# Twelve seven-product pairs instead of sixteen in a two-row-block encoder layer, with the norm's squares, the first loads and the last rows in another order

## The chip, the cores and the metric

The kernel runs on one core of a Trainium2 chip, as one program in one launch. The metric is the device time of that program in microseconds (us), and lower is better. A run of this kernel can be told from another when they differ by about 0.2%, some 2.7 us.

## The reference

The layer works on x, 256 positions of 2048 channels, in float32:

```python
def mixer_block(x, g_norm, w_in, ln_g, ln_b, w_s, b_s, rpb, w_branch, w_out):
    h = rms_norm(x, g_norm)
    proj = h @ w_in
    uv, qkv, gates = jnp.split(proj, [2 * GM_WIDTH, 2 * GM_WIDTH + 3 * NA_WIDTH], axis=-1)
    ...
    return x + merged @ w_out

def conv_ffn(x, g_norm, w_up, conv_k, conv_b, w_down):
    h = rms_norm(x, g_norm)
    up = h @ w_up
    ...
    gate, val = jnp.split(up, 2, axis=-1)
    return x + (jax.nn.silu(gate) * val) @ w_down

def reference(x, norm_mix, ...):
    ...
    return rms_norm(x, norm_final)
```

What matters here is that every matrix product is float32, that the mixer's norm scales its rows by a factor which is known only when the squares of x are summed, that the feed-forward part has 5504 inner channels (43 tiles of 128), and that a last norm over all 2048 channels of a row comes before the output.

## The kernel before, in words

**Products.** TensorE (PE) takes reduced-precision operands, so each float32 operand is split into a high and a low part: ScalarE (ACT) writes the high part (`high`, line 244) and VectorE (DVE) the rest (`low`, line 247). A product is then three matmuls, high by high, low by high and high by low (`three_products`, lines 381 to 383; `spread_products`, lines 366 and 372, is the same for weights that stand still). The weights come as one stream of packed pieces of 128 x 1024 from HBM, all on SyncE's (SP's) queue, through five raw buffers (`RAW`), and four, later six, buffers of split weights (`UNITS`). Piece i + 4 is prepared at the beginning of step i (`begin`, `prepare`) when a buffer is free. The first 16 pieces also carry a 128 x 256 part of x, turned, in four buffers of their own.

**Order of the work.** Each engine executes what the program emits, in that order. A step i of the loop emits the loads that have a free buffer, the splits of the pieces ahead, the tasks that were put down for step i with `at`, and then the matmuls of piece i. So a split that stands behind a task on ACT or DVE waits for that task.

**Start.** The group `vg` (16 pieces, `first_step`, lines 398 to 401) makes v of the gMLP branch in four PSUM banks; at its end four gelu activations (line 634) read these banks, with the rows' factor of the norm as their scale. That factor comes from `x_norm`, put down for step 15, after eight square sums (line 1163) in steps 11 to 14, of x rows that are loaded behind piece 15. Then follow the groups `u` (two of eight pieces).

**Feed-forward.** It is done in two blocks of 22 and 21 inner tiles. In a block, the `up` groups make pairs of inner tiles; a convolution, the gate and a split into high and low parts follow on DVE and ACT, as tasks of the next steps. Then two `down` groups (j = 0, 1), each of 22 or 21 pieces, multiply them by `w_down` into 1024 columns each.

**Seven products for eight.** Two neighbouring pieces of a `down` group are a 2 x 2 block product (two inner tiles by two column halves, for two halves of the positions): eight products. For some pairs (`FF_SEVEN`: 1, 3, 5 and 7, counted in pairs from the group's beginning, in both blocks) it is done with seven, by sums and differences of the operands. The sums of the weights are made by DVE: four additions of 128 x 512 (lines 293, 300, 303 and 304), between the splits. `sums` emits a pair's preparation in four parts, `one` to `four`, and `plan` puts the last two behind the first part of the next piece. The split operands are a half (128 x 512, `halves`), and three units: `b`, the second piece as it came, `t` and `s`, sums. The first step of a pair (9 matmuls) uses the half and `t`, the second (12 matmuls) uses `s` and `b`. After the last pair `combine` (line 475) folds four banks into x2, all at once.

**End.** The last three pieces of the last group are done block by block (`LAST`): for each of the four 128 x 512 blocks of the result all its remaining matmuls, so that blocks are complete one after the other. `finish` (line 1098) adds the last block of a row half to x2, sums its squares, makes the norm's factor, scales the 2048 columns in five parts and stores them; first for rows 0 to 127, then for rows 128 to 255.

Of the kernel before, what the change touches and what calls it, by code (L numbers as in the profile page):

```python
# [46 lines left out]
FF_SEVEN = (1, 3, 5, 7)  # L47
LAST = 3
# [101 lines left out]
def trunk_kernel(ctx, tc, x, weights, vectors, ln_g, ln_b, w_s_turned, b_s, rpb, norm_final, out):  # L150
# [62 lines left out]
    def load():  # L213
        while n_loaded[0] < len(pieces):
# [66 lines left out]
    def sums(i):  # L281
# [4 lines left out]
        def one():  # L286
# [3 lines left out]
            r0 = raw[i][0]  # L290
# [4 lines left out]
        def two():  # L295
            r0, r1 = raw[i][0], raw[i + 1][0]
            hb, lb = unit((i, "b"))
            ht, lt = unit((i, "t"))
            high(hb, r1)
            nc.vector.tensor_add(r0[:, c1], r0[:, c1], r1[:, c1])  # L300
            high(ht, r0)
            low(lb, r1, hb)
            nc.vector.tensor_add(r1[:, c1], r1[:, c1], r0[:, c0])
            nc.vector.tensor_add(r1[:, c0], r1[:, c0], r1[:, c1])
            low(lt, r0, ht)
            raw_done(i)

        def three():
            r1 = raw[i + 1][0]
            h, l = unit((i, "s"))  # L310
            high(h, r1)

        def four():
            r1 = raw[i + 1][0]
            h, l, _ = units[i, "s"]
# [3 lines left out]
        return one, two, three, four  # L319
# [4 lines left out]
    def plan():  # L324
        late = None
        i = 0
        while i < len(pieces):
            if i in seven:
                one, two, three, four = sums(i)
                if late:  # L330
                    queue.append((i, 1, 0, late[0]))
                queue.append((i, 0, 1, one))
                if late:
                    queue.append((i, 0, 0, late[1]))
                queue.append((i + 1, 2, 0, two))
                late = (three, four)
                i += 2
                continue
            if late:
                queue.append((i, 1, 0, late[0]))  # L340
            queue.append((i, 1, 0, split_piece(i)))
            if late:
                queue.append((i, 0, 0, late[1]))
            late = None
            i += 1
        if late:
            queue.extend([(i, 1, 0, late[0]), (i, 0, 0, late[1])])
# [37 lines left out]
    def first_step(key, acts, done):  # L385
# [3 lines left out]
        def step(i):  # L389
# [13 lines left out]
            if last:  # L403
                for b in range(NT):
                    for c in range(2):
                        done(box["ps"][2 * b + c], b, c, i + 1)
                        free(box["ps"][2 * b + c])
# [36 lines left out]
    def wide_step(key, acts, sevens, rest, done, by_block=0):  # L444
# [9 lines left out]
        while n < size:  # L454
            if n in firsts:
                uses += [1, 5, 7, 6, 2, 3, 4]
# [18 lines left out]
        def combine():  # L475

            nu, nv = (fx["p"].tile([128, 512], F32, name=f"comb{n}") for n in range(2))
            nc.scalar.activation(nu, p(1), AF.Copy)
            rest(0, 0, nu, OP.add)
            nc.vector.tensor_sub(nu, nu, p(6))  # L480
            nc.vector.tensor_sub(nv, nu, p(7))
            rest(0, 1, nu, OP.subtract)
            rest(0, 1, p(5), OP.add)
            rest(1, 0, nv, OP.add)
            rest(1, 1, nv, OP.subtract)
            rest(1, 1, p(5), OP.add)
            free(p(1), p(6), p(7), p(5))

        def step(i):
            n = i - n0  # L490
            c0, c1 = slice(0, 512), slice(512, 1024)
            if n in firsts:
                k = tiles[n]
                h, l, _ = halves[i]
                ht, lt, _ = units[i, "t"]
                S = sevens(k)
                product(1, acts(k, 0), (h, l))
                product(5, S[0], (ht[:, c0], lt[:, c0]))
                product(7, S[2], (ht[:, c1], lt[:, c1]))
                unit_done((i, "t"))  # L500
                half_free.append(halves.pop(i)[2])
            elif n - 1 in firsts:
                k = tiles[n - 1]
                hb, lb, _ = units[i - 1, "b"]
                hs, ls, _ = units[i - 1, "s"]
                S = sevens(k)
                product(6, S[1], (hs[:, c1], ls[:, c1]))
                product(2, acts(k + 1, 0), (hb[:, c0], lb[:, c0]))
                product(3, S[3], (hb[:, c1], lb[:, c1]))
                product(4, acts(k + 1, 1), (hs[:, c0], ls[:, c0]))  # L510
                unit_done((i - 1, "b"))
                unit_done((i - 1, "s"))
                if n - 1 == firsts[-1]:
                    combine()
# [6 lines left out]
            elif n == size - 1:  # L521
                for c in range(2):
                    for b in range(NT):
                        for m in range(size - by_block, size):
                            h, l, _ = units[n0 + m]
                            cs = slice(c * 512, (c + 1) * 512)
                            product(OUT[b, c], acts(tiles[m], b), (h[:, cs], l[:, cs]))
                        done(p(OUT[b, c]), b, c, i + 1)
                        free(p(OUT[b, c]))
# [27 lines left out]
    ck = vec[:, 2 * KD:].rearrange("p (j f) -> p j f", j=4)  # L557
    nc.scalar.dma_start(gmix, vectors[:, :KD])
# [68 lines left out]
    def ev_vg():  # L627
        def done(p, t, j, i):
            G = gm_pool["p"]
            if "v" not in gm_pool:  # L630
                gm_pool["v"] = [G.tile([128, GMW], F32, name=f"vg{b}") for b in range(NT)]
                gm_pool["sum"] = const.tile([128, NT, 2], F32, name="vsum")
                at(i + 1, ln_stats)
# [667 lines left out]
```

## Time and profile before

| | |
|---|---|
| three runs | 1343.62, 1345.53 and 1345.92 us; median 1345.53 us |
| the profiled execution's own time | 1345.03 us |
| its span in the trace | 1342.9 us |
| mean clock granted to TensorE | 0.993 |
| PE busy | 1312.0 us (98%) |
| DVE busy | 966.9 us (72%) |
| ACT busy | 736.0 us (55%) |
| the `down` groups | 854.06 to 972.99 us, and 1206.82 us to the last matmul |

The times of the trace count from the span's beginning, and 2.1 us of the profiled execution lie outside the span. A row of the timeline gives start, duration, engine, line and operation, output and inputs (buffer numbers left out) and, in brackets, how long the engine stood idle before it and what ended that. Rows of matmuls overlap: what a matmul costs in a stream is the distance of the starts, not the duration shown.

### The profile page before, as it was taken

How to read it: one execution, taken by the hardware profiler on the slowest of the kernel's cores; microseconds unless marked ns; L12 is line 12 of the kernel's file. 1: busy time of each engine (PE TensorE's matmuls, PEld its weight loads, DVE VectorE, ACT ScalarE, POOL GpSimd, SP SyncE). 2: the span in 40 equal slices, each digit the busy share in tenths (PEclk: the TensorE clock that was granted, in tenths of full speed). 3: DMA queues.
4: the chain of work that ended last, by engine and by line, in shares of the span. 5: the costliest groups of instructions: out<-in, count | busy, mean ns of one | idle time of the engine just before them, and what ended most of it. 6: DMA issues, size and time to landing. Idle time of an engine off the chain costs nothing.

```text
span 1342.9 us, 18498 instructions
## 1 busy us (share of the span) xinstructions
PE 1312.0 (98%) x6766; PEld 1117.6 (83%) x6766; DVE 966.9 (72%) x1397; ACT 736.0 (55%) x1082; POOL 96.5 (7%) x190
## 2 busy tenths in 40 slices
PE   9999999999999999999999999989999999998986
PEld 7788888888888888888888888878888888886865
DVE  6387667777564546555878787899867878779886
ACT  6655567576544444545655555554545555555453
POOL 0411065430000000000000000000000000000000
PEclk9999999999999999999999999999999999999988
DMA  8866776645666668565656565466756565655552
GB/s 301 315 188 195 212 221 188 198 155 184 188 187 190 193 193 265 193 197 167 191 189 189 192 191 189 145 204 190 248 177 199 180 199 183 187 167 172 202 172 95
DMA packets 74187, 261.41 MB, mean 195 GB/s; under 512 B 9584, under 2 KB 11248, under 8 KB 73584
## 3 DMA queue, kind: packets, MB, share of 16 engines
q1 hardware_dynamic: 69984, 252.40, 59.3%
q0 software_dynamic: 3680, 7.30, 2.1%
q8 instruction: 53, 0.87, 0.3%
q10 hardware_dynamic: 432, 0.53, 0.1%
q14 instruction: 38, 0.31, 0.1%
HBM read 256.00 MB, written 2.10 MB: 192 GB/s over the span
## 4 chain that ended last, share of the span: by engine, by line
PE 91%; DVE 4%; ACT 2%; issue 1%; DMA 1%; SPq 0%; DVEq 0%; ACTq 0%
PE bank L366 29%; PE bank L372 15%; PE bank L383 14%; PE bank L381 14%; PE bank L382 14%; DVE wlo L247 2%; PE bank L398 1%; PE bank L401 1%; PE bank L399 1%; ACT whi L244 1%; PE bank L835 1%; DMA start<-in_weights_dram 0%; DMA wraw<-in_weights_dram 0%; ACT junk L1074 0%; DVE x L969 0%
## 5 line engine op out<-in xcount | busy, mean ns | idle before, releaser
L247 DVE TENSOR_TENSOR wlo<-wraw,whi 128x1024 fp32r<-128x1024 f32 (+1 forms) x470 | 564.4, 1217 | 226.9 <-ACT whi L244 219.3
L244 ACT ACTIVATE whi<-wraw 128x1024 fp32r<-128x1024 f32 (+1 forms) x470 | 484.2, 1046 | 273.7 <-PE bank L382 151.6
L366 PE MATMUL bank<-h,whi 128*128 128x512 f32 x1760 | 424.8, 392 | 0.0
L366 PEld LDWEIGHTS bank<-h,whi 128*128 128x128 f32 x1760 | 323.9, 189 | 62.0
L372 PEld LDWEIGHTS bank<-h,wlo 128*128 128x128 f32 x1760 | 226.8, 191 | 11.5 <-DVE wlo L247 2.5
L372 PE MATMUL bank<-h,wlo 128*128 128x256 f32 x1760 | 231.4, 284 | 2.3 <-DVE wlo L247 2.3
L383 PE MATMUL bank<-wlo,a 128*128 128x512 f32 x312 | 123.4, 396 | 11.9 <-DVE wlo L247 11.9
L381 PE MATMUL bank<-whi,h 128*128 128x512 f32 x320 | 126.0, 394 | 0.0
L381 PE MATMUL bank<-whi,a 128*128 128x512 f32 x312 | 122.8, 393 | 3.1 <-ACT whi L244 2.9
L383 PE MATMUL bank<-wlo,h 128*128 128x512 f32 x320 | 124.8, 390 | 0.0
L382 PE MATMUL bank<-whi,h 128*128 128x512 f32 x320 | 124.7, 390 | 0.0
L382 PE MATMUL bank<-whi,a 128*128 128x512 f32 x312 | 122.2, 392 | 0.0
L1025 ACT ACTIVATE tc<-ta,vec 128x256 f32<-128x256 f32 x86 | 47.1, 594 | 88.0 <-DVE ta L1023 88.0
L701 DVE TENSOR_TENSOR ta<-bank,tb 128x256 f32<-128x256 f32 x110 | 39.0, 416 | 64.1 <-ACT tb L699 64.1
L699 ACT ACTIVATE tb<-bank 128x256 f32<-128x256 f32 x110 | 36.2, 384 | 89.1 <-PE bank L366 83.3
L383 PEld LDWEIGHTS bank<-wlo,a 128*128 128x128 f32 x312 | 59.1, 189 | 27.5 <-DVE wlo L247 15.4
L381 PEld LDWEIGHTS bank<-whi,a 128*128 128x128 f32 x312 | 59.2, 190 | 16.2 <-ACT whi L244 3.9
L383 PEld LDWEIGHTS bank<-wlo,h 128*128 128x128 f32 x320 | 60.1, 188 | 12.7
L381 PEld LDWEIGHTS bank<-whi,h 128*128 128x128 f32 x320 | 60.2, 188 | 12.2
L382 PEld LDWEIGHTS bank<-whi,h 128*128 128x128 f32 x320 | 60.2, 188 | 11.9
L382 PEld LDWEIGHTS bank<-whi,a 128*128 128x128 f32 x312 | 59.1, 189 | 12.3
L1028 DVE SCALAR_TENSOR_TENSOR tc<-ta,vec,tc 128x255 f32<-128x255 f32 x86 | 41.4, 481 | 14.4 <-ACT tc L1025 14.4
(169 smaller groups left out, 1321.5 us busy)
## 6 DMA issues: line engine op xcount, KB each, us to landing
wraw<-in_weights_dram SPq DMA_DIRECT2D x446, 512.0 KB, 4.4
start<-in_weights_dram SPq DMA_DIRECT2D x15, 640.0 KB, 6.0
xs<-in_x_dram SPq DMA_DIRECT2D x2, 1024.0 KB, 9.2
vw<-va POOLq DMA_DIRECT2D x32, 64.0 KB, 5.9
x<-in_x_dram POOLq DMA_DIRECT2D x2, 1024.0 KB, 9.7
wraw<-in_weights_dram SPq DMA_DIRECT2D x8, 256.0 KB, 2.7
run<-in_rpb_dram POOLq DMA_DIRECT2D x64, 31.2 KB, 3.9
h<-in_norm_final_dram POOLq DMA_DIRECT2D x4, 256.0 KB, 5.6
```

The lines of the kernel that those rows point to most:

```text
L244: nc.scalar.activation(h, w, AF.Copy)
L247: nc.vector.tensor_sub(l, w, h.bitcast(F32))
L366: nc.tensor.matmul(p, h[:, c:c + 128], acts(2 * n + k), start=n == 0 and k == 0, stop=last and k == tiles - 1)
L372: nc.tensor.matmul(p[:, :T], l[:, c:c + 128], acts(2 * n + k)[:, 0, :], start=False, stop=False)
L381: nc.tensor.matmul(p, xh, wh, start=start, stop=False)
L382: nc.tensor.matmul(p, xl, wh, start=False, stop=False)
L383: nc.tensor.matmul(p, xh, wl, start=False, stop=stop)
L398: nc.tensor.matmul(p, xh, h[:, cs], start=n == 0, stop=False)
L699: nc.scalar.activation(t, p[:, T:], AF.Copy)
L701: nc.vector.tensor_add(a, p[:, :T], t)
L1025: nc.scalar.activation(v, u, AF.Identity, scale=ck[:, 1, ch:ch + 1], bias=ck[:, 3, ch:ch + 1])
L1028: nc.vector.scalar_tensor_tensor(v[:, 1:], u[:, :T - 1], ck[:, 0, ch:ch + 1], v[:, 1:], op0=OP.mult, op1=OP.add)
```

## The change

Line numbers in the parts that follow the diff are those of each kernel; in the changed kernel `low` is line 248 and `high` line 245.

- `FF_SEVEN` gives each block its own three pairs: (3, 5, 7) in the first, (2, 4, 6) in the second. With two groups per block that is 12 pairs instead of 16; pairs 0 and 1 of a group are now never among them.
- A pair's preparation has three parts in plain order: `plain` (the half and `b`, as they came), `summed` (all four additions, then `t`) and `last` (`s`). The first step of a pair now uses the half and `b` (products 1, 2, 3), the second uses `t` and `s` (products 5, 7, 6, 4).
- `combine` is spread over the three steps behind the last pair. The tiles of split activations with and without sums have their own names.
- x's rows are loaded ahead of pieces 8 and 9 instead of behind piece 15. The squares are eight tasks of steps 6 to 13, one each, and `x_norm` is put down for step 14. The four gelu activations are put down for steps 16 and 17, two each.
- The loads of the first pieces are emitted ahead of the norm's weights; piece 0 comes in three parts, and its part of x is issued by ACT, ahead of the norm's weights on that queue.
- `LAST` is 4. `finish` is written anew: what is left of rows 0 to 127 is scaled among the steps of rows 128 to 255, two multiplications by the norm's weights go to GpSimd (POOL), and the output goes out in seven parts.

```diff
-FF_SEVEN = (1, 3, 5, 7)
-LAST = 3
+FF_SEVEN = ((3, 5, 7), (2, 4, 6))
+LAST = 4
...
-            for c0, c1 in ((0, 768), (768, 1280)) if i == 0 else ((0, size),):
-                nc.sync.dma_start(w[:, c0:c1], bass.AP(tensor=weights.tensor, offset=weights.offset + off + c0,
+            for c0, c1 in ((T, 768), (0, T), (768, 1280)) if i == 0 else ((0, size),):
+                queue = nc.scalar if (i, c0) == (0, 0) else nc.sync
+                queue.dma_start(w[:, c0:c1], bass.AP(tensor=weights.tensor, offset=weights.offset + off + c0,
...
+        def plain():
+            r0, r1 = raw[i][0], raw[i + 1][0]
             slot = half_free.pop(0)
             h, l = (slot[0].tile([128, 512], F32R, name=f"half_{p}{slot[1]}") for p in ("hi", "lo"))
             halves[i] = (h, l, slot)
+            hb, lb = unit((i, "b"))
             high(h, r0[:, c0])
+            high(hb, r1)
             low(l, r0[:, c0], h)
+            low(lb, r1, hb)
+
+        def summed():
+            r0, r1 = raw[i][0], raw[i + 1][0]
+            ht, lt = unit((i, "t"))
             nc.vector.tensor_add(r0[:, c0], r0[:, c0], r0[:, c1])
             nc.vector.tensor_add(r0[:, c1], r0[:, c1], r1[:, c1])
             nc.vector.tensor_add(r1[:, c1], r1[:, c1], r0[:, c0])
             nc.vector.tensor_add(r1[:, c0], r1[:, c0], r1[:, c1])
+            high(ht, r0)
             low(lt, r0, ht)
             raw_done(i)
...
+                queue.extend([(i, 1, 1, plain), (i + 1, 1, 0, summed), (i + 1, 1, 0, last)])
...
-                for c in range(2):
-                    for b in range(NT):
-                        for m in range(size - by_block, size):
+                for b, c in ((0, 0), (1, 0), (0, 1), (1, 1)):
+                    u = OUT[b, c]
+                    for m in range(size - by_block, size):
...
+    load()
     nc.scalar.dma_start(gmix, vectors[:, :KD])
...
+            for n in range(4):
+                at(i + n // 2, lambda n=n: gelu(n // 2, n % 2))
+            at(i + 2, ln_stats)
...
+        v = x2[:, t, 1536:]
+        nc.vector.tensor_add(v, p, v)
+        nc.scalar.activation(junk, v, AF.Square, accum_out=ss[:, t, 3:4])
+        fin["y", t] = hpool.tile([128, 512], F32, name=f"h{t}")
+        if t == 0:
+            nc.vector.tensor_mul(fin["y", 0], v, fin["g", 3])
+            root(0)
+        else:
+            scaled(0, 0, 512, nc.vector, nc.sync)
+            scaled(0, 512, 1024, nc.vector, nc.sync)
+            root(1, lambda: (nc.vector.tensor_mul(fin["y", 1], v, fin["g", 3]),
+                             scaled(0, 1024, 1536, nc.scalar, nc.sync)))
+            scaled(1, 640, 1536, nc.scalar, nc.scalar)
+            scaled(1, 0, 640, nc.vector, nc.sync)
+            scaled(1, 1536, 2048, nc.vector, nc.sync)
+            scaled(0, 1536, 2048, nc.vector, nc.sync)
...
-        preload[16 + t] = [lambda t=t: load_rows(t)]
+        preload[8 + t] = [lambda t=t: load_rows(t)]
...
-    for c in range(4):
-        at(11 + c, lambda c=c: x_stats(c))
-    at(15, x_norm)
+    for n in range(8):
+        at(6 + n, lambda n=n: x_stats(n // 4, n % 4))
+    at(14, x_norm)
```

`scaled` multiplies a stretch of a row half by the norm's factor on the engine named and stores it by the queue named; `root` makes the factor, as before, with one more multiplication at its end.

Three places show what moved. The first is DVE at the beginning of the second block's first `down` group (`half_lo` and `wlo` are low parts, `wraw` the raw weights that are added, `ta` the sums of the last `up` group, `full` its gated result). Before:

```order
1142 L247 TENSOR_TENSOR half_lo_11373<-wraw_11297,half_hi_11372 128x512
1143 L293 TENSOR_TENSOR wraw_11297<-wraw_11297 128x512
1144 L300 TENSOR_TENSOR wraw_11297<-wraw_11297,wraw_11313 128x512
1145 L247 TENSOR_TENSOR wlo_11386<-wraw_11313,whi_11385 128x1024
1146 L303 TENSOR_TENSOR wraw_11313<-wraw_11313,wraw_11297 128x512
1147 L304 TENSOR_TENSOR wraw_11313<-wraw_11313 128x512
1148 L247 TENSOR_TENSOR wlo_11388<-wraw_11297,whi_11387 128x1024
1149 L701 TENSOR_TENSOR ta<-bank_11263,tb 128x256
1150 L701 TENSOR_TENSOR ta<-bank_11264,tb 128x256
1151 L247 TENSOR_TENSOR wlo_11419<-wraw_11337,whi_11418 128x1024
1152 L247 TENSOR_TENSOR wlo_11416<-wraw_11313,whi_11415 128x1024
```

The same place in the changed kernel:

```order
1124 L248 TENSOR_TENSOR wlo_11344<-wraw_11268,whi_11343 128x1024
1125 L248 TENSOR_TENSOR wlo_11358<-wraw_11284,whi_11357 128x1024
1126 L696 TENSOR_TENSOR ta<-bank_11234,tb 128x256
1127 L696 TENSOR_TENSOR ta<-bank_11235,tb 128x256
1128 L248 TENSOR_TENSOR half_lo_11381<-wraw_11308,half_hi_11380 128x512
1129 L248 TENSOR_TENSOR wlo_11383<-wraw_11324,whi_11382 128x1024
1130 L301 TENSOR_TENSOR wraw_11308<-wraw_11308 128x512
1131 L302 TENSOR_TENSOR wraw_11308<-wraw_11308,wraw_11324 128x512
1132 L303 TENSOR_TENSOR wraw_11324<-wraw_11324,wraw_11308 128x512
1133 L304 TENSOR_TENSOR wraw_11324<-wraw_11324 128x512
1134 L248 TENSOR_TENSOR wlo_11405<-wraw_11308,whi_11404 128x1024
1135 L248 TENSOR_TENSOR wlo_11413<-wraw_11324,whi_11412 128x1024
```

Two pieces of a plain kind (tiles 2 and 3) now stand where the first pair stood, and the pair comes behind the `up` group's sums; inside the pair the additions stand together, behind both plain splits.

The second place is ACT around the end of the first group (`junk,xsq` are the squares, `n_s` is a step of the norm's factor, `vg` the gelu activations, `whi` high parts). Before:

```order
39 L244 ACTIVATE whi_484<-wraw_376 128x1024
40 L1163 ACTIVATE junk,xsq<-xs 128x512 x2
41 L244 ACTIVATE whi_505<-wraw_379 128x1024
42 L583 ACTIVATE n_s<-n_a 128x2
43 L634 ACT_TABLE_LOAD
44 L634 ACTIVATE vg_533,vsum<-bank_188,n_r 128x512
45 L634 ACTIVATE vg_533,vsum<-bank_189,n_r 128x512
46 L634 ACTIVATE vg_534,vsum<-bank_190,n_r 128x512
47 L634 ACTIVATE vg_534,vsum<-bank_191,n_r 128x512
48 L244 ACTIVATE whi_542<-wraw_382 128x1024
49 L244 ACTIVATE whi_568<-wraw_385 128x1024
```

In the changed kernel:

```order
44 L1175 ACTIVATE junk,xsq<-xs 128x512
45 L245 ACTIVATE whi_487<-wraw_380 128x1024
46 L573 ACTIVATE n_s<-n_a 128x2
47 L245 ACTIVATE whi_518<-wraw_383 128x1024
48 L245 ACTIVATE whi_539<-wraw_386 128x1024
49 L624 ACT_TABLE_LOAD
50 L624 ACTIVATE vg_534,vsum<-bank_189,n_r 128x512
51 L624 ACTIVATE vg_534,vsum<-bank_190,n_r 128x512
52 L245 ACTIVATE whi_567<-wraw_389 128x1024
53 L624 ACTIVATE vg_535,vsum<-bank_191,n_r 128x512
54 L624 ACTIVATE vg_535,vsum<-bank_192,n_r 128x512
55 L245 ACTIVATE whi_591<-wraw_485 128x1024
```

The factor's step now stands two splits ahead of the gelu activations, not right ahead of them, and a split stands between the two halves of these.

The third place is DVE at the end of the program, where the last block of rows 0 to 127 is done and that of rows 128 to 255 follows (`x` is x2, `b` and `r`, `e` the factor, `a` the mean square). Before:

```order
1272 L1108 TENSOR_SCALAR e_12284<-e_12284 128x1
1273 L1116 TENSOR_SCALAR x_4960<-x_4960,r_12282,e_12284 128x256
1274 L1118 TENSOR_TENSOR b_12290<-r_12282,e_12284 128x1
1275 L1116 TENSOR_SCALAR x_4960<-x_4960,r_12282,e_12284 128x512
1276 L1116 TENSOR_SCALAR x_4960<-x_4960,r_12282,e_12284 128x256
1277 L1116 TENSOR_SCALAR x_4960<-h_12279,r_12282,e_12284 128x512
1278 L969 TENSOR_TENSOR x_4960<-bank_11904,x_4960 128x512
1279 L1102 TENSOR_TENSOR h_12313<-x_4960,h_11567 128x512
1280 L1104 TENSOR_SCALAR a_12315<-ss_146,part 128x1
```

In the changed kernel:

```order
1245 L1123 TENSOR_TENSOR b_12238<-r_12235,e_12237 128x1
1246 L1098 TENSOR_TENSOR x_4961<-bank_11860,x_4961 128x512
1247 L1132 TENSOR_SCALAR x_4961<-x_4961,b_12238 128x512 x2
1248 L1116 TENSOR_SCALAR a_12264<-ss_156,part_12215 128x1
1249 L1107 TENSOR_TENSOR h_12259<-x_4961,h_11540 128x512
1250 L1120 RECIPROCAL r_12265<-q_12266 128x1
...
1253 L1123 TENSOR_TENSOR b_12268<-r_12265,e_12267 128x1
1254 L1132 TENSOR_SCALAR x_4961<-x_4961,b_12268 128x640
1255 L1132 TENSOR_SCALAR x_4961<-h_12259,b_12268 128x512
1256 L1132 TENSOR_SCALAR x_4961<-h_12232,b_12238 128x512
```

The addition that reads the very last block now comes right behind the first factor, ahead of all scaling of the first rows.

More of the change, by code (lines that the diff above doesn't have):

```diff
@@ L311, in three @@
             high(h, r1)
-        def four():
-            r1 = raw[i + 1][0]
-            h, l, _ = units[i, "s"]
             low(l, r1, h)
             raw_done(i + 1)
-        return one, two, three, four
+        return plain, summed, last
     seven = {}
@@ L324, in plan @@
     def plan():
-        late = None
         i = 0
@@ L328, in plan @@
             if i in seven:
[L329 to L336, printed above, removed]
-                i += 2
[L338 to L347, printed above, removed]
+                plain, summed, last = sums(i)
+                queue.extend([(i, 1, 1, plain), (i + 1, 1, 0, summed), (i + 1, 1, 0, last)])
+                i += 2
+            else:
+                queue.append((i, 1, 0, split_piece(i)))
+                i += 1
     def prepare(n):
@@ L1012, in ev_up @@
         blk, pair = pair_of(f0)
-        with_sums = nb == 2 and pair in FF_SEVEN
+        with_sums = nb == 2 and pair in FF_SEVEN[blk]
         def done(ps, i):
@@ L1061, in down_acts @@
         n = {(0, 0): 1, (0, 1): 0, (1, 0): 2, (1, 1): 3}[(f - FF_BLOCKS[blk][0]) % 2, b]
-        if pair in FF_SEVEN and not whole:
+        if pair in FF_SEVEN[blk] and not whole:
             n -= 1
```

162 lines of the change are left out of this document (78 added, 84 removed).

## Prediction

> **What bounds the kernel now.** I read the busy shares first, then PE's list of waits, then PE's timeline in the stretches that the change touches. The page's first part:
>
> ```profile
> PE 1312.0 (98%) x6766; PEld 1117.6 (83%) x6766; DVE 966.9 (72%) x1397; ACT 736.0 (55%) x1082; POOL 96.5 (7%) x190
> ```
>
> PE is the bound, so time can come from three things only: fewer matmuls, fewer stalls of PE, and a shorter end behind its last matmul. PE's three costliest waits (sum, times, longest):
>
> ```profile
> PE bank L383 <- DVE wlo L247: 11.9, 7, 2.6
> PE bank L381 <- ACT whi L244: 2.9, 1, 2.9
> PE bank L372 <- DVE wlo L247: 2.3, 1, 2.3
> ```
>
> The first two are waits of the `down` groups (`bank<-wlo,a`), the third lies in group `u`. The sums hide what a wait costs beside itself, so I read PE's timeline of the `down` groups:
>
> ```profile
> 854.06 0.39 PE L381 MATMUL bank<-whi,a 128*128 128x512 f32 x1
> 871.51 0.39 PE L383 MATMUL bank<-wlo,a 128*128 128x512 f32 x1
> 875.37 0.50 PE L383 MATMUL bank<-wlo,a 128*128 128x512 f32 x1 [2.61 <-DVE wlo L247]
> 972.99 1.98 PE L366 MATMUL bank<-h,whi 128*128 128x512 f32 x8
> 1206.82 0.39 PE L381 MATMUL bank<-whi,a 128*128 128x512 f32 x1
> 1279.02 0.49 PE L381 MATMUL bank<-whi,a 128*128 128x512 f32 x1 [2.94 <-ACT whi L244]
> 1282.36 0.80 PE L383 MATMUL bank<-wlo,a 128*128 128x512 f32 x1 [2.61 <-DVE wlo L247]
> 1282.96 0.63 PE L381 MATMUL bank<-whi,a 128*128 128x512 f32 x1
> 1286.80 0.42 PE L381 MATMUL bank<-whi,a 128*128 128x512 f32 x1
> 1330.82 0.39 PE L383 MATMUL bank<-wlo,a 128*128 128x512 f32 x1
> ```
>
> From 854.06 to 871.51 there are 77 starts: (871.51 - 854.06)/77 = 0.2266 us is a matmul of 512 columns in a stream. The first block has 22 x 12 x 2 - 8 x 3 = 504 of them, 114.2 us, but takes 972.99 - 854.06 = 118.9: **4.7 us** are stalls. The second has 480; the 479 before the last would take 108.6 us, but 1330.82 - 1206.82 = 124.0: **15.4 us** are stalls. Between 1282.96 and 1286.80, behind two waits, nine distances take 0.427 each, about twice 0.2266: the waits are followed by matmuls at half speed. The Trainium skill ("TensorE: Matmul & The Clock Gate", Part 1) describes a free-running activity window of about 3.4 us by which the clock is halved and restored; rows 1282.96 to 1286.80 agree, and the single 2.61 at 875.37 shows no such stretch.
>
> **The change part by part.**
>
> *Four pairs fewer.* Each pair saved 3 matmuls: 12 x 0.2266 = **+2.7 us**, certain.
>
> *Stalls in the `down` groups.* What makes the weights late is DVE and ACT, whose work for a pair is:
>
> ```profile
> 881.95 1.22 DVE L247 TENSOR_TENSOR wlo<-wraw,whi 128x1024 fp32r<-128x1024 f32 x1
> 886.75 1.06 ACT L244 ACTIVATE whi<-wraw 128x1024 fp32r<-128x1024 f32 x1 [0.85 <-DMA wraw<-in_weights_dram]
> 936.26 0.69 DVE L303 TENSOR_TENSOR wraw<-wraw,wraw 128x512 f32<-128x512 f32 x1
> 936.99 0.69 DVE L304 TENSOR_TENSOR wraw<-wraw 128x512 f32<-128x512 f32 x1
> 1222.17 0.43 DVE L1037 TENSOR_TENSOR full<-tc 128x256 f32<-128x256 f32 x1
> 1270.15 0.68 DVE L969 TENSOR_TENSOR x<-bank,x 128x512 f32<-128x512 f32 x1
> 1278.05 0.69 DVE L1089 TENSOR_TENSOR x<-x,h 128x512 f32<-128x512 f32 x1 [0.85 <-ACT junk L1074]
> wraw<-in_weights_dram SPq DMA_DIRECT2D x446, 512.0 KB, 4.4
> ```
>
> The last row is from the DMA issues (KB each, median us from issue to landing). In plain order a pair costs DVE four additions of about 0.7, then `t`'s low part 1.2. A pair's second raw buffer is one that the pair before gave back when its `t` was done. From the end of that low part (881.95 + 1.22 = 883.17) to the next piece in that buffer (886.75) took 3.6; then the high part of `b` 1.1, its low part 1.2, four additions 2.8, `t` 1.2: 9.85 us from `t` to `t`. PE needs for a pair (21 matmuls, 4.76) and two plain steps (2.72 each) 10.2. So in the steady state the pairs just keep up, by 0.35 us; by the median landing of 4.4 instead of 3.6 the loop takes 10.7 and each of the eight following pairs lacks 0.5. I take the lower, for it is measured in this very place, and keep 4 us for the range.
>
> At a group's beginning the cover is the plain steps ahead of the first pair. In the first block (pairs at 3, 5, 7, so six plain steps, 16.3 us) I find at least 2.4 us of slack. In the second (pairs at 2, 4, 6: four steps, 10.9 us) it is tight. Group 0: DVE is done with the `up` group's product at about 1222.6 (row 1222.17), after which half, `b`, sums and `t` must follow; added up they come 0.1 to 0.15 late in two places, so 0.3 in all. Group 1 starts at T1, when the four sums into x2 begin, each followed by a square on ACT and a product: rows 1270.15 to 1278.05 make this chain 8.5 us, so it ends at T1 + 8.7. Behind it come the half's low part 0.6, 0.4 of waiting for ACT, `b` 1.2, additions 2.8 and `t` 1.2: T1 + 14.9. PE has done four plain steps and a pair's first 9 matmuls at T1 + 12.9 and needs the low part at 13.4: a wait of 1.5 to 1.7. Together **+2.0** (0.5 to 6). The old stalls of 4.7 + 15.4 go: **-20.1**. That includes the 2.94 at 1279.02, which was the same chain with the first pair only one step behind the group's start.
>
> *The beginning.* PE and ACT around the first `u` group:
>
> ```profile
> 57.41 1.11 PE L372 MATMUL bank<-h,wlo 128*128 128x256 f32 x8
> 60.80 1.59 PE L372 MATMUL bank<-h,wlo 128*128 128x256 f32 x8 [2.28 <-DVE wlo L247]
> 65.62 2.10 PE L366 MATMUL bank<-h,whi 128*128 128x512 f32 x8
> 67.55 2.07 PE L372 MATMUL bank<-h,wlo 128*128 128x256 f32 x16
> 69.46 3.82 PE L366 MATMUL bank<-h,whi 128*128 128x512 f32 x16
> 58.42 2.01 ACT L244 ACTIVATE whi<-wraw 128x1024 fp32r<-128x1024 f32 x2
> ```
>
> From 57.41 to 67.55 passed 10.1 us. The same work in a stream is a row of x16 at L372 (69.46 - 67.55 = 1.91), one at L366 (16 x 0.2266 = 3.63) and four small transposes, about 0.4: 5.9. The other **-4.2** are the wait of 2.28 and slow matmuls behind it. ACT came to the two splits at 58.42 only, behind squares, factor, table load and four gelus. In the new order squares and factor are done steps earlier and a split stands between the gelus, so this goes. What comes in their place are x's rows, 2 MB ahead of pieces 8 and 9:
>
> ```profile
> 7.33 0.39 PE L398 MATMUL bank<-whi,h 128*128 128x512 f32 x1
> 9.08 0.50 PE L398 MATMUL bank<-whi,h 128*128 128x512 f32 x1 [0.23 <-ACT whi L244]
> 21.46 0.51 ACT L258 ACTIVATE h<-start,vec 128x256 fp32r<-128x256 f32 x1 [0.36 <-DMA start<-in_weights_dram]
> start<-in_weights_dram SPq DMA_DIRECT2D x15, 640.0 KB, 6.0
> xs<-in_x_dram SPq DMA_DIRECT2D x2, 1024.0 KB, 9.2
> 38.00:40.00 2.00, 2.00 (x10) 1.67 (x9) 0.49 (x1) 0.72 (x2) 0.00 (x0) 1.00 1.03 424
> ```
>
> Piece 8 landed at 21.46. Piece 9 will have 2 MB of rows and its own 0.64 MB, some 2.75 MB with small loads, behind that point: at the 424 GB/s of the window 38 to 40 us 6.5 us, so it lands at about 28, its low part is ready 2.7 later, at 31, and PE needs it at 9.08 + 8 x 2.72 + 0.9 = 31.75. At the mean of the first nine pieces (5.9 MB by 21.46, some 300 GB/s with the start-up) it lands at 30.5 and PE waits 1.5. The Trainium skill ("DMA: Bandwidth & Descriptors", on bandwidth) gives about 358 GB/s of HBM per core; the row of 424 is above it, and by 358 piece 9 would land at 29.1 and just be in time. ACT now issues a load ahead of its first split; I take 0.4 later for PE's start and nothing for the rows: **+0.4** (0 to 3).
>
> *The end.* DVE's two rows, then the windows (the last columns are the DMA share and GB/s):
>
> ```profile
> 1333.91 0.68 DVE L969 TENSOR_TENSOR x<-bank,x 128x512 f32<-128x512 f32 x1
> 1336.51 0.41 DVE L1116 TENSOR_SCALAR x<-x,r,e 128x256 f32<-128x256 f32 x1
> 1339.00:1340.00 1.00, 0.00 (x0) 0.00 (x0) 0.00 (x0) 0.00 (x0) 0.00 (x0) 0.50 1.03 367
> 1340.00:1341.00 1.00, 0.00 (x0) 0.00 (x0) 0.00 (x0) 0.00 (x0) 0.00 (x0) 0.50 0.82 299
> ```
>
> PE was done at 1330.82 + 0.23 = 1331.05 (T), but the last sum began at 1333.91, 2.7 late behind the scaling of rows 0 to 127; scaling followed 2.6 later, and the span ended at 1342.9 = T + 11.85. Now the sum comes at T + 0.2 and scaling of the last rows at T + 3.45. But more output is then left: about 1.28 MB, at 367 GB/s 3.5 us from T + 4.7, so T + 8.25, and 2.1 behind the last transfer as before: T + 10.35. The queue takes back half of the 2.7: **-1.4** (-0.5 to -2.5). The two products on POOL have over 3 us of cover; 128 x 512 took DVE 0.69 (row 1278.05), and at three times that they would still fit.
>
> *Sum.* 2.7 - 20.1 + 2.0 - 4.2 + 0.4 - 1.4 = -20.6. The profiled execution took 1345.03 (span 1342.9 and 2.1 outside), so 1324.4; the median of the runs is 0.5 above it: **1325.0 us**, -1.5%. A measurement can tell 0.2%, about 2.7 us, from no change.
>
> **The rivals.**
> A, the forecast, 1321 to 1329: chance 0.64.
> B, the pairs do not quite keep up: landing at 4.4 gives 8 x 0.5 = 4, and later first pairs 2 more: 1331. For it speaks the slack of only 0.35; against it that fewer pairs leave DVE and the queue freer. 0.17.
> C, the start gives some back: x's rows hold piece 9 by 1.5, or PE starts later and slowly, together 2.5 more: 1327.5. The skill's window of 3.4 us, named above, would at most cost half of itself, 1.7, if the later start misses one; that rests on the page, the 2.5 on the rows. 0.12.
> E, the waits move rather than vanish: the second block still shows two waits close together with slow matmuls between; half of 20.1 stays: 1335. 0.04.
> D, slower: the following pairs wait for their landings. If the stream landed in 6.85 us or more where a pair returns its buffer, the loop would be 13.1, each of the eight pairs would lack 2.9 = 23 us and 1348 would be reached; it decides from a landing of 6.5. For it, x's rows took 9.2 when the DMA was full (1.03); against it 4.4 is the median of 446 and 3.6 was seen here. 0.03.
>
> **How the numbers follow.** The range 1320.5 to 1332 holds A, C and B, with the bounds of -2.5 at the end and +4 for the loop; E and D lie outside. Faster by over 0.2% are A, B, C and E, less a little for their neighbours of D: 0.95; the same 0.02; slower 0.03.
>
> **What the profile will show.** If right: PE's waits in `down` fall to about 2 us, the longest at the fifth step of the last group, no distances of 0.43 there; no wait near 58 us; none near 31 us; the last sum on DVE right behind PE's last matmul; a span near 1322. Wrong would be: waits at each following pair (B, D), a wait for piece 9 or slow matmuls till beyond 8 us (C), or an end that is still 12 us behind PE.

## The result, and the profile after

The changed kernel took 1331.59 us (median of four runs, 1330.95 to 1332.03) against 1345.48 us before: a ratio of 0.9899, 95% interval 0.9882 to 0.9916. That is 13.9 us less. The forecast was 20.5 less, 1325.0 us; the measured time lies in the range (1320.5 to 1332.0), at its upper end, and 6.6 us above the point. Where the 6.6 us went is the question of the rest.

The page's first part and PE's waits, as shown of before:

```profile
PE 1316.1 (99%) x6778; PEld 1116.5 (84%) x6778; DVE 945.4 (71%) x1362; ACT 728.8 (55%) x1072; POOL 100.3 (8%) x192
```

```profile
PE bank L561 <- POOL ident masks.py:199: 1.4, 1, 1.4
PE bank L381 <- DVE h L257: 1.0, 1, 1.0
PE bank L366 <- DVE wlo L248: 0.8, 1, 0.8
```

The waits of `down` and of `u` are gone as forecast, all but one of 0.8 us. With fewer waits than foreseen the kernel is still 6.6 us slower than foreseen: PE is busy for that time, so its matmuls take longer. PE's timeline of the `down` groups shows it:

```profile
854.86 0.39 PE L364 MATMUL bank<-whi,a 128*128 128x512 f32 x1
857.58 0.40 PE L364 MATMUL bank<-whi,a 128*128 128x512 f32 x1
863.19 0.39 PE L364 MATMUL bank<-whi,a 128*128 128x512 f32 x1
971.85 2.02 PE L349 MATMUL bank<-h,whi 128*128 128x512 f32 x8
1206.16 0.39 PE L364 MATMUL bank<-whi,a 128*128 128x512 f32 x1
1318.95 0.39 PE L366 MATMUL bank<-wlo,a 128*128 128x512 f32 x1
```

Twelve matmuls from 854.86 to 857.58 take 0.2267 each (start to start), as in a stream of the kernel before. The next 24, to 863.19, take 5.61/24 = 0.2338 each, 3% more, with no wait between them. The window of that stretch (the last three columns are granted clock, DMA share and GB/s) shows a granted clock of 1.00:

```profile
854.00:870.00 16.00, 16.00 (x71) 13.10 (x70) 14.08 (x23) 8.61 (x14) 0.00 (x0) 1.00 0.29 108
```

It is not one stretch: the slow steps come back in each group, always with certain buffers, and full-speed steps lie between them, so a clock that fell for a while is not the reason. When the program's order of matmuls is laid beside the trace, the 276 matmuls of `down` that have a split unit of the right side of SBUF (units 4 and 5) and an `a` of the left side stand 0.2334 apart on average; those with both on the left stand 0.227 apart. The same happens where the change touches nothing. The first matmuls with `y` (branch products) and with `m` (`out` products), of before and of after:

```profile
339.58 0.39 PE L381 MATMUL bank<-whi,y 128*128 128x512 f32 x1
517.18 0.39 PE L381 MATMUL bank<-whi,m 128*128 128x512 f32 x1
```

```profile
336.56 0.39 PE L364 MATMUL bank<-whi,y 128*128 128x512 f32 x1
516.68 0.39 PE L364 MATMUL bank<-whi,m 128*128 128x512 f32 x1
```

The stretch between them took 177.60 us before and 180.12 after, with the same instructions. All stages of the two profiled executions, in us (the sum is the difference of the spans, 13.8):

| stage | before | after | difference |
|---|---|---|---|
| to the end of the first group | 50.03 | 51.17 | +1.14 |
| from there to line 595/585 in group `u` (transposes) | 15.23 | 11.13 | -4.10 |
| to the first `y` | 274.32 | 274.26 | -0.06 |
| first `y` to first `m` | 177.60 | 180.12 | +2.52 |
| first `m` to the `up` groups | 90.61 | 91.42 | +0.81 |
| `up`, first block | 246.27 | 246.76 | +0.49 |
| `down`, first block | 118.93 | 116.99 | -1.94 |
| `up`, second block | 233.83 | 234.31 | +0.48 |
| `down`, second block | 124.23 | 113.02 | -11.21 |
| behind the last matmul | 11.86 | 9.96 | -1.90 |

The beginning and the end, to be set beside the rows of before:

```profile
5.60 0.77 PE L381 MATMUL bank<-whi,h 128*128 128x512 f32 x1 [0.98 <-DVE h L257]
...
9.61 0.46 PE L382 MATMUL bank<-whi,h 128*128 128x512 f32 x1
...
51.17 1.98 PE L349 MATMUL bank<-h,whi 128*128 128x512 f32 x8
58.55 2.08 PE L355 MATMUL bank<-h,wlo 128*128 128x256 f32 x16
64.60 2.08 PE L355 MATMUL bank<-h,wlo 128*128 128x256 f32 x16
```

```profile
1260.14 0.69 DVE L964 TENSOR_TENSOR x<-bank,x 128x512 f32<-128x512 f32 x1
1268.06 0.69 DVE L1084 TENSOR_TENSOR x<-x,h 128x512 f32<-128x512 f32 x1 [0.85 <-ACT junk L1071]
1273.45 4.77 DVE L248 TENSOR_TENSOR wlo<-wraw,whi 128x1024 fp32r<-128x1024 f32 x4
1319.38 0.68 DVE L1098 TENSOR_TENSOR x<-bank,x 128x512 f32<-128x512 f32 x1
1322.48 0.55 DVE L1132 TENSOR_SCALAR x<-x,b 128x640 f32<-128x640 f32 x1
```

From 58.55 to 64.60 passed 6.05 us where it had been 10.14. PE's last matmul ends at 1318.95 + 0.23 = 1319.18 (T); the last sum begins at T + 0.20 and the scaling of the last rows at T + 3.30, as forecast.

### The profile page after: what moved, and what is told of

Read it like the earlier page. It is cut to its first block, busy times and chain, and to the rows that moved or that the text cites. A ratio compares the mean times of both kernels' runs of the same rounds, so it can differ in the third digit from the quotient of the medians.

```text
span 1329.1 us, 18475 instructions
## 1 busy us (share of the span) xinstructions
PE 1316.1 (99%) x6778; PEld 1116.5 (84%) x6778; DVE 945.4 (71%) x1362; ACT 728.8 (55%) x1072; POOL 100.3 (8%) x192
## 4 chain that ended last, share of the span: by engine, by line
PE 95%; DVE 3%; DMA 1%; ACT 1%; issue 0%; ACTq 0%; DVEq 0%
PE bank L349 30%; PE bank L355 16%; PE bank L364 14%; PE bank L366 14%; PE bank L365 14%; PE bank L381 1%; PE bank L382 1%; PE bank L384 1%; DVE wlo L248 1%; DMA wraw<-in_weights_dram 1%; PE bank L830 1%; ACT whi L245 0%; PE bank L882 0%; DMA vec<-in_vectors_dram 0%; PE bank L704 0%
## 5 line engine op out<-in xcount | busy, mean ns | idle before, releaser
L366 PE MATMUL bank<-wlo,a 128*128 128x512 f32 x248 | 97.2, 392 | 0.8 <-DVE wlo L248 0.8
L364 PE MATMUL bank<-whi,a 128*128 128x512 f32 x248 | 97.2, 392 | 0.0
L365 PE MATMUL bank<-whi,a 128*128 128x512 f32 x248 | 97.2, 392 | 0.0
L366 PEld LDWEIGHTS bank<-wlo,a 128*128 128x128 f32 x248 | 46.6, 188 | 11.6 <-DVE wlo L248 1.3
L364 PEld LDWEIGHTS bank<-whi,a 128*128 128x128 f32 x248 | 46.6, 188 | 10.3
L365 PEld LDWEIGHTS bank<-whi,a 128*128 128x128 f32 x248 | 46.6, 188 | 10.3
```

The costliest lines, as they stand in the source:

```text
L364: nc.tensor.matmul(p, xh, wh, start=start, stop=False)
L365: nc.tensor.matmul(p, xl, wh, start=False, stop=False)
L366: nc.tensor.matmul(p, xh, wl, start=False, stop=stop)
```

## The experiments

**Where the buffers lie.** The theory that came out of the profile: the slow matmuls are a side effect of the new `finish`. The kernel before has one small tile `part` there, the changed kernel two, `part0` and `part1`, and each takes 32 bytes of every partition. By the program's allocation everything behind them on the left side of SBUF (units 0 to 3, `h`, `m`, `a`, `s`) moves by 32 bytes; what is allocated from the right end (`y`, units 4 and 5, the half) stays. The slow steps are those whose moving operand (the one that streams through) is in unit 4 or 5 while the stationary one (`a`) is on the left, or the other way round (`y` right, the units left). The addresses are those of the program's allocation; no trace holds them. I added an unused tile, `const.tile([128, n], F32, name="pad")`, ahead of the buffers.

e1, the changed kernel and 32 bytes:

```diff
     one = const.tile([128, 1], F32)
+    const.tile([128, 8], F32, name="pad")
```

> The changed kernel with one unused 32-byte tile ahead of the weight buffers, and nothing else. In the changed kernel finish has two small tiles (part0, part1) where there was one, and everything behind them on the left side of SBUF lies 32 bytes further; the buffers on the right side (x2, two of six units, halves, y) do not. Theory P (place): a matmul is 3% slower when its two operands differ by 32 in their address modulo 64 (0.2334 against 0.2270 us in the changed kernel's down groups; none differs in the kernel before). 1320 of 4676 matmuls of 512 columns differ in the changed kernel; here none does, so about 7.4 us go: 1324.2 us, all distances 0.2266. Rival R (run or regulation): the 3% come and go with the clock, the heat or the load of the chip, whatever the addresses: 1331.6 us and distances of 0.233 again. Rival S (stalls): the 7 us are waits after all: 1331.6 us.

Measured: 1327.33 us (ratio to before 0.9866, 95% interval 0.985 to 0.9881). Not one instruction that PE waits for was changed, and the time is lower, so R and S fall. But the gain fell short of the 1324.2 expected, and the steps in unit 4 and 5 were as slow as ever: modulo 64 is not the rule.

e3, both sides at 0 modulo 64 by moving the right side:

```diff
+    keep("edge", "right").tile([128, 8], F32, name="edge")
     ypool, y_st = pool("yT", "right")
```

> The changed kernel with a 32-byte tile at the far end of the right side of SBUF, so that the buffers there move by 32 bytes and both sides lie at 0 modulo 64 (in the kernel before both lie at 32). Theory P, the difference of the two operands counts: as the 32-byte tile on the left, 1324.2 us. A variant of P, that 32 modulo 64 is the good place for one of the operands: no better than the changed kernel, 1331.6 us or more. Rivals R and S: 1331.6 us.

Measured: 1327.47 us (0.9864, 0.9851 to 0.9878), the same as e1: it is the difference of the two sides that counts, not which side is moved.

e4, 64 bytes (`[128, 16]`):

> The changed kernel with an unused tile of 64 bytes at the same place: the left side moves by 64 bytes, so the differences modulo 64 stay as they are in the changed kernel (1320 matmuls of 512 columns differ). Theory P: 1331.6 us, as the changed kernel. If any move of the buffers changes the time (another distance, bank boundaries): something else, either way.

Measured: 1332.57 us (0.9902, 0.9888 to 0.9915), as expected; moving things is no gain in itself.

e2, the kernel before with the tile of 32 bytes:

> The kernel before with the unused 32-byte tile: its left side now lies at 0 modulo 64, its right side at 32; 1296 matmuls of 512 columns differ, none did. Theory P: about 7 us slower than the kernel before, 1352.5 us; where PE waits anyway the loss may be covered, so 1350 to 1353. Rivals R and S: 1345.5 us.

Measured: 1351.38 us against 1345.93 (1.0045, 1.0033 to 1.0058): 5.5 us slower by an unused tile. The expected 7 was too much: by stages `y` lost 2.52, `m` 0.81, the first `down` 1.03, but the `up` groups only 0.49 and 0.46, and the second `down`, where PE waits anyway, 0.02.

e5 and e6, 96 and 224 bytes (`[128, 24]`, `[128, 56]`):

> The changed kernel with an unused tile of 96 bytes ahead of the weight buffers: the left side of SBUF then lies at 96 modulo 256, the right side at 224, so they agree modulo 128 and not modulo 256. With 32 bytes of padding (agreement modulo 64 alone) the kernel took 1327.3, and its matmuls of down with the two units on the right side still stood at 0.2335 us. Theory P128 (agreement modulo 128 counts): all distances 0.2267, about 4 us less than with 32 bytes, 1323.3 us. Theory P256 (it is modulo 256 or more, as in the kernel before, where both sides are at 224): no better than 32 bytes, 1327 us. Rival X (the two units are slow for another reason, such as who writes them): 1327 us here and with 224 bytes.

> The changed kernel with an unused tile of 224 bytes: both sides of SBUF lie at 224 modulo 256, as in the kernel before. Theories P128 and P256: 1323.3 us, down groups of 115.9 and 111.5 us instead of 117.0 and 112.8, every distance 0.2267. Rival X: 1327 us.

Measured: 1332.34 us (0.9896, 0.988 to 0.9913) and 1325.99 us (0.9848, 0.9833 to 0.9863). So P128 and X fall; of what was tried only agreement modulo 256 gives full speed. No theory had foreseen a time as long as e5's (1327 was the longest expected), and e6 is 2.7 above its expected 1323.3: against e1 the stages of `y`, `m` and the first `down` gained 3.1 us, but the `up` groups, which were faster in e1, gave back 1.7. Steps 1 and 2 of the first `down` group are the 24 matmuls in units 4 and 5; their beginning and end in e1 were 854.62 and 860.22; in e5 and then in e6:

```profile
858.23 0.40 PE L364 MATMUL bank<-whi,a 128*128 128x512 f32 x1
863.82 0.39 PE L364 MATMUL bank<-whi,a 128*128 128x512 f32 x1
```

```profile
853.94 0.39 PE L364 MATMUL bank<-whi,a 128*128 128x512 f32 x1
859.38 0.39 PE L364 MATMUL bank<-whi,a 128*128 128x512 f32 x1
966.82 1.98 PE L349 MATMUL bank<-h,whi 128*128 128x512 f32 x8
1200.65 0.39 PE L364 MATMUL bank<-whi,a 128*128 128x512 f32 x1
1313.37 0.39 PE L366 MATMUL bank<-wlo,a 128*128 128x512 f32 x1
```

And PE's waits in `down` in e6:

```profile
PE bank L366 <- DVE wlo L248: 1.4, 2, 0.7
```

5.59/24 = 0.2329 in e5, 5.44/24 = 0.2267 in e6. All the places, by address modulo 256 (left side, right side):

| kernel | left, right | first `y` to first `m` | a matmul in units 4 and 5 with `a` | time |
|---|---|---|---|---|
| before | 224, 224 | 177.60 | 0.2267 | 1345.48 to 1346.31 |
| e6 | 224, 224 | 177.60 | 0.2267 | 1325.99 |
| e1 | 32, 224 | 178.45 | 0.2333 | 1327.33 |
| e3 | 0, 192 | 178.46 | 0.2333 | 1327.47 |
| e5 | 96, 224 | 179.93 | 0.2329 | 1332.34 |
| e4 | 64, 224 | 180.22 | 0.2342 | 1332.57 |
| after | 0, 224 | 180.12 | 0.2338 | 1331.59 |
| e2 (kernel before) | 0, 224 | 180.12 | 0.2336 | 1351.38 |

In e6 the untouched stages are back at the times of before to 0.01 us (177.60, 90.61, 246.27, 233.83). With the places equal the change is worth 1346.31 - 1325.99 = 20.3 us.

Both sides were made equal at one place only, 224; is it the agreement that counts, or that place? The first twelve matmuls of the same `down` group answer this, for both of their operands lie on the left. They take 2.72/12 = 0.2267 each with the left side at 0 (after), at 32 (e1), at 64 (e4) and at 96 (e5). So operands that agree are fast at each of these places.

**The load order at the start.** e7, on top of e6:

```diff
+    nc.scalar.dma_start(gmix, vectors[:, :KD])
     load()
-    nc.scalar.dma_start(gmix, vectors[:, :KD])
```

> The padding of 224 bytes, and the load of the mixer norm's weights again ahead of piece 0's part of x on ACT's queue. In the changed kernel these weights landed at about 5.1 instead of 4.5 us, the first matmul came at 5.60 instead of 5.01 and the end of the first group 1.1 later. Theory Q (that queue order costs the 1.1 us): 1.1 us less than with the padding alone, 1322.2 us. Rival: the part of x, now second, is as late as the weights were: no change.

Measured: 1326.25 us (0.9846, 0.9829 to 0.9864), no change against e6. In single profiles the first group ended at 50.76 (e7) and 51.44 (e6), but over the eight profiled executions with the new order it ends anywhere from 49.86 to 51.44, and over three with e7's order (e7, e8, e12) from 50.01 to 50.94. Whether the order costs some tenths stays open; 1.1 is not shown.

**More pairs.** e8, on top of e7:

```diff
-FF_SEVEN = ((3, 5, 7), (2, 4, 6))
-LAST = 4
+FF_SEVEN = ((3, 5, 7, 9), (2, 4, 6, 8))
+LAST = 3
```

> As the one before (padding of 224 bytes, norm's weights first), with a fourth pair in each group: pairs (3, 5, 7, 9) and (2, 4, 6, 8), and LAST of 3, since the last pair's pieces would be among the last four. 12 matmuls fewer: 2.7 us. Theory K (preparation in plain order keeps up: loop 9.85 against 10.2 us): 2.7 us less, 1319.5 us, PE's waits in down still under 1 us. Rival W (the fourth pair brings waits again, or its spread sums delay the end): between 1 us less and 3 us more, waits of 2 us and more in the fourth pairs.

Measured: 1331.10 us (0.9886, 0.9871 to 0.9901), 4.9 slower than e7: rival W by its mechanism, though more than the 3 us that W allowed. PE's costliest waits, its last matmul and the sum behind it:

```profile
PE bank L364 <- DVE x L959: 1.8, 1, 1.8
...
PE bank L364 <- ACT whi L245: 1.3, 1, 1.3
PE bank L366 <- DVE wlo L248: 1.0, 2, 0.7
PE bank L364 <- DVE x L965: 0.8, 1, 0.8
```

```profile
1313.96 0.39 PE L366 MATMUL bank<-wlo,a 128*128 128x512 f32 x1
1318.79 0.68 DVE L1099 TENSOR_TENSOR x<-bank,x 128x512 f32<-128x512 f32 x1
```

In the first block the preparation kept up, in the second not quite (the 1.3 and the 1.0). Above all the folding of the four banks (L959) came at the group's end: the next group waited for banks, and the last sum began 4.6 us behind the last matmul (1314.19) instead of 0.2, so the end took 14.3 us instead of 9.9. The edit has `LAST` at 3 as well, and how much of the longer end is due to that was not tried.

**Number and place of the pairs, or their order.** e9, on top of e6, has the old pairs in the new order of preparation ("order" stands here for all that the new kernel does otherwise with a pair, the spread folding too):

```diff
-FF_SEVEN = ((3, 5, 7), (2, 4, 6))
+FF_SEVEN = ((1, 3, 5, 7), (1, 3, 5, 7))
```

> The padding of 224 bytes (1326.0 us, both sides of SBUF agree), with the pairs where they were before, (1, 3, 5, 7) in both blocks, but prepared in the new plain order. 12 matmuls fewer than the twelve pairs of the change: 2.7 us. Theory N (number and place of the pairs end the waits): the first pair stands behind two plain steps again; in the last group its sum t is ready about 12.4 us behind the group's start and PE needs it at 8, so some 4 us of waits there, more in group 0 behind the up group's product, and slow matmuls behind them: 1331 to 1341 us. Rival O (the plain order ends them): no waits, 1323.3 us.

e10 is the kernel before, in its old order of preparation, with `FF_SEVEN = (3, 5, 7)`:

> The kernel before with FF_SEVEN = (3, 5, 7) instead of (1, 3, 5, 7) in both blocks, and its old order of preparation. Four pairs fewer: 2.7 us more of matmuls. Theory N: the stalls of the down groups (4.7 and 15.4 us) go all but 1 or so: 1345.9 + 2.7 - 19 = 1329.5 us. Rival O (the old order brings the waits): at least half of the stalls stays, 1338 us or more.

Measured: e9 1332.49 us (0.9899, 0.9885 to 0.9912), e10 1333.56 us (0.9908, 0.9895 to 0.9922). The waits of PE that bear on it, e9 and then e10:

```profile
PE bank L364 <- DVE x L965: 3.6, 3, 1.3
PE bank L366 <- DVE wlo L248: 1.6, 3, 0.7
...
PE bank L364 <- DVE ta L697: 1.1, 1, 1.1
```

```profile
PE bank L383 <- DVE wlo L247: 2.5, 3, 1.1
```

The first block of e9, from 850.42 to 964.66, took 114.24 us: 504 x 0.2266 = 114.2, not one stall, where the old order had 4.7 with the same pairs. Its second block took 118.36 against 108.8: 9.6 of stalls, where the old order had 15.4. So in the first block the plain order alone ends the stalls (O), in the second the place is needed (N). N's reason was only a part of it there: the largest wait, the 3.6, is not for weights but for banks that the sums into x2 (L965) had yet to free. Besides, e9's end took 12.5 us instead of 9.9. e10 says the same from the other side: with the old order and later pairs 1.3 us of stalls stay in the first block (116.92 against 115.6) and 3.1 in the second (113.19 against 110.1). Both parts do work, and neither theory was right alone.

**The squares.** e11, on top of e6:

```diff
-        preload[8 + t] = [lambda t=t: load_rows(t)]
+        preload[16 + t] = [lambda t=t: load_rows(t)]
...
-        at(6 + n, lambda n=n: x_stats(n // 4, n % 4))
-    at(14, x_norm)
+        at(11 + n // 2, lambda n=n: x_stats(n // 4, n % 4))
+    at(15, x_norm)
```

> The padding of 224 bytes, with x's rows loaded behind piece 15 again, two squares in each of the steps 11 to 14 and the norm's factor in step 15, as before; the gelus stay split two and two. Theory Q2 (the early squares and factor end the wait in group u): the 10.1 us between the two marks in u come back from 7.2 or so, 4.1 us more in all: 1330.1 us. Rival: the split between the gelus is enough: 1326 us or 1 more.

Measured: 1325.60 us (0.9848, 0.9834 to 0.9861), the same as e6. PE's two marks in `u`, and ACT between them:

```profile
57.24 2.08 PE L355 MATMUL bank<-h,wlo 128*128 128x256 f32 x16
63.29 2.08 PE L355 MATMUL bank<-h,wlo 128*128 128x256 f32 x16
```

```profile
51.60 1.04 ACT L245 ACTIVATE whi<-wraw 128x1024 fp32r<-128x1024 f32 x1
54.64 0.68 ACT L625 ACTIVATE vg<-bank,n_r 128x512 f32<-128x512 f32 x1
55.30 1.06 ACT L245 ACTIVATE whi<-wraw 128x1024 fp32r<-128x1024 f32 x1
56.25 0.68 ACT L625 ACTIVATE vg<-bank,n_r 128x512 f32<-128x512 f32 x1
```

Still 6.05 us between the marks. What ends the wait in `u` is the new place of the gelus: one split now stands ahead of them (51.60) and one between two and two (55.30), where the kernel before came to both at 58.42. With late squares the factor is in time for that too. The two splits were not tried one by one. The early squares are worth nothing that this measurement shows.

**A better version.** e12, on top of e7, has `FF_SEVEN = ((3, 5, 7), (3, 5, 7))`:

> The padding of 224 bytes and the norm's weights first (1326.2 us), with pairs (3, 5, 7) in the second block too. There PE still waited 0.7 for the sums of the second pair of the last group and 0.7 to 1.3 for a low part that stands behind the folding of the four banks on DVE. Theory K2: with one plain pair more ahead both waits go, about 1.5 us less: 1324.7 us. Rival W: the folding comes so late that the end behind the last matmul (9.9 us) grows, as with four pairs (14.3): 1327 to 1330 us.

Measured: 1323.99 us (0.9835, 0.9821 to 0.9848), the fastest of all, 7.6 us under the changed kernel. It is 2.3 under e7, less than the 2.7 by which two runs can be told apart, so this step rests on the rows. All waits of PE that are left, and the end:

```profile
PE bank L562 <- POOL ident masks.py:199: 1.4, 1, 1.4
PE bank L381 <- ACT whi L245: 0.6, 1, 0.6
```

```profile
1200.16 0.39 PE L364 MATMUL bank<-whi,a 128*128 128x512 f32 x1
1310.10 0.39 PE L366 MATMUL bank<-wlo,a 128*128 128x512 f32 x1
1311.87 0.68 DVE L1099 TENSOR_TENSOR x<-bank,x 128x512 f32<-128x512 f32 x1
```

The second block's `down` groups take 110.17 us, 486 x 0.2266 = 110.1, without a stall (K2, which expected 1.5 us); in e6 they took 112.95. Of these 2.8 us the end gives back 1.3, since the last sum now begins 1.54 behind the last matmul (1310.33) instead of 0.2: a little of W. Old pairs in the first block beside these in the second (e9's 114.24 there instead of 115.60) would be another 1.4 us, an estimate from these rows; that was not run.

## Why the prediction was right or wrong, point by point

- **Four pairs fewer, +2.7:** right. The first block without stalls takes 114.24 with sixteen pairs in all (e9) and 115.60 with twelve (e6): 1.36, twice.
- **Stalls of `down`, -20.1, with 2.0 left:** right in size. In e6, where the places agree, 115.60 is 510 x 0.2266 to 0.03, and 112.95 leaves 2.8. Wrong was the place of the 2.0. I let the chain of sums in the last group start 0.2 behind the group's start; it started 1.84 ahead of it (1260.14 against 1261.98 in the changed kernel), because the first block of the result is complete after three of the last step's twelve matmuls. `t`'s low part was done about 1274.7 (the first of the four from 1273.45), 12.7 behind the start and not 14.9, and PE did not wait there. In e6 it waited 0.7 in the second pair and 0.7 for a low part behind the folding.
- **The start, -4.2 and +0.4:** the size of the first was right (-4.1), its cause only half: the new place of the gelus did it, with the squares as late as before (e11). The first group ended 1.14 later instead of 0.4: the first matmul came 0.59 later, and the half-speed matmuls went on to 9.61, where they had ended by 7.33 before, which is the other 0.55. That is the loss that the prediction took from the Trainium skill's page on the clock gate ("TensorE: Matmul & The Clock Gate", Part 1) as the skill's share of rival C, half a window at most; this profile agrees in the size and in the distances (8.33 to 8.75, 9.18 to 9.61), but its granted clock reads 1.00 from 5.60 to 9.60, so the clock itself is not shown. The page also calls it variable from run to run, and so it is here: the first group's end moves by 1.6 us among profiles of the same order, so how much of the 1.14 is the change can't be said. x's rows ahead of pieces 8 and 9 brought no wait (rival C's first half falls): behind its first 24 matmuls the group takes 38.08 us in all fourteen profiles.
- **The end, -1.4:** right, -1.9. The steps at T + 0.20 and T + 3.30 came as worked out; the span ended at T + 9.96 instead of T + 10.35.
- **Rivals:** B's time (1331) is what was measured, but not by B's mechanism: in the changed kernel PE waited at no following pair. In e6, at full matmul rate, it did at one of the eight, by 0.7: there ACT got the next piece 5.4 us behind the end of `t`'s low part (about 1269.2) and not 3.6, so the slack of 0.35 is as thin as B said, but B's 4 us did not come. D and E did not occur.

```profile
1274.59 1.06 ACT L245 ACTIVATE whi<-wraw 128x1024 fp32r<-128x1024 f32 x1 [2.95 <-DMA wraw<-in_weights_dram]
```

- **What failed** is a step that the prediction made without saying so: "a matmul of 512 columns costs 0.2266 us in a stream" was carried from the old program to the new, as if it belonged to the instruction. It belongs to the instruction and the places of its two operands. Stage by stage against e6 this cost 2.52 (`y`), 0.81 (`m`), 0.49 and 0.48 (`up`), 1.39 and 0.07 (`down`, where e6 waits more in turn): 5.8 us, and 1331.59 - 1325.99 = 5.6 in the times. Without this loss the sum of -20.6 would have held: with equal places (e6) the change gives -20.3. That the measured time still lies in the range, 0.4 under its upper bound, is luck, for no term and no rival of the prediction held this loss.

The Trainium skill ("TensorE: Matmul & The Clock Gate", Part 2, the step-by-step section) says that TensorE reads the streamed operand and the next weights through two independent ports, so that loading weights takes no read bandwidth from the running matmul. No run here tests that sentence. What they show beside it is that the same stream takes 0.2267 or 0.2338 us a matmul depending on where the two operands lie; why, and whether reading them together is the cause, no run here shows.

## What to carry to other kernels

When a trace after a change shows PE busy and late at the same time, measure the distance of its matmuls per buffer before looking for waits, and compare a stage that the change does not touch. A small tile added anywhere can move every large buffer behind it; for matmuls of 512 columns keep the two operands at the same address modulo 256, for instance by a padding tile, recheck it whenever a small tile comes or goes, and measure it, for shorter matmuls went the other way here (below). And a stall that two edits could end is told apart only by making each alone: here order and place shared the work in `down`, and of two edits at the start only one did any.

## What the runs showed of the hardware that I had not expected

- A matmul of 512 columns takes 0.2267 us when its two operands have the same address modulo 256, and up to 0.2342 when they have not, at a granted clock of 1.00. Differences of 32, 64, 96 and 128 between the sides were seen; all cost about 3% where the moving operand was in units 4 and 5 and `a` stood still. With `y` standing still on the right a difference of 64 cost about a third of it (178.45 against 177.60 and 180.12).
- In the `up` groups the sign can turn: with the sides 64 apart (e1) they took 245.42 us, 0.85 less than at equal places (246.27). There the moving operand is `h` and the units stand still. With the buffers that the program gives each piece laid beside the traces, it is the matmuls of 256 columns that gain: with their unit on the right they stand 0.1158 apart in e1 and 0.1197 in e6 (456 of them), while those of 512 columns take as long in both (0.229 and 0.228). Why is open.
- An unused tile of 32 bytes makes the kernel before 5.5 us slower (e2), twice what the measurement can tell.
